# Two sets of retention tiles, and the gated merges as a phase of their own, in an eight-core retention and Hyena layer

## The chip, the cores and the metric

The kernel runs on the eight NeuronCores of one Trainium2 chip, the same program on each, with no communication between cores. Time is device time of the slowest core, in microseconds (us). Two states occur, in the kernels before and after and in 12 of the 14 experiments: in some executions the cores of one die (cores 0 to 3 or 4 to 7) get a lower clock and take some per cent longer.

Engines: PE is TensorE's matmul, PEld its weight load, DVE is VectorE, ACT is ScalarE, POOL is GpSimd, SP is the SyncE queue (it only issues DMAs here). In the traces of before and after, DVE's, ACT's and POOL's instructions run in the order in which the program issues them: on all eight cores the sequences agree by operation and size (1331, 872 and 227 instructions after the change, DMA issues included). PE's matmuls do so too (5770 after the change) on the six cores of which no records are missing. All windows below are of core 0.

## The reference, cut to what matters

One layer: normalise and modulate (`h`), one wide projection, retention (four heads), a Hyena convolution, a gated merge with output projection, then a SwiGLU FFN.

```python
h = rmsnorm(x, norm1) * (1 + scale1) + shift1
proj = h @ w_in
q, k, v, g, hu, g_ret, g_hy = jnp.split(proj, splits, axis=-1)
o, s_f, s_b = bidir_retention(qh, kh, vh, gamma_f, gamma_b, s0_fwd, s0_bwd)
y_ret = (jax.nn.silu(g) * head_groupnorm(o)) @ w_ret_o
# ... Hyena branch: z ...
y_hy = z @ w_hy_o
mix = jax.nn.sigmoid(g_ret) * y_ret + jax.nn.sigmoid(g_hy) * y_hy
x = x + gate1 * (mix @ w_out)
h2 = rmsnorm(x, norm2) * (1 + scale2) + shift2
a, bgt = jnp.split(h2 @ w_ffn_in, 2, axis=-1)
x = x + gate2 * ((jax.nn.silu(a) * bgt) @ w_ffn_out)
```

Each core has three tiles of 512 rows to bring through this: two of context (`xc`) and one of its own sample rows (`xs`). It also needs keys and values of the other half of its sample's rows, for the states. `h` is used twice: by q, k, v, g, and by the gates `g_ret`, `g_hy`.

## The kernel before

All weights of the retention phase are in SBUF together: `WR` (q, k, v, g and both gates), `WRO`, `WHO`, `WO`. There is one working set, so one `HT_R` (the transposed, modulated `h` of a tile) and one Q, K, V.

`make_hT` makes hT in 16 small stages for four blocks of 128 rows: st1 loads rows and sums squares (DVE, ACT), st2 scales (DVE), st3 transposes on PE and evicts by turns with DVE and ACT. With `defer` the stages go to a queue, and `fill(n)` puts n of them into the program wherever it is called.

```python
stages = [L(st1, 0), L(st1, 1), L(st2, 0), L(st3, 0, 0), L(st3, 0, 1), L(st1, 2), L(st2, 1), L(st3, 1, 0), L(st3, 1, 1),
          L(st1, 3), L(st2, 2), L(st3, 2, 0), L(st3, 2, 1), L(st2, 3), L(st3, 3, 0), L(st3, 3, 1)]
# st3 with hf == 1 ends with after_blk(blk): for a retention tile, K, V (and SG = silu(g)) of that block, 8 matmuls each
```

A tile then goes: Q and K by heads (`ret_rest`), retention (`ret_st`), merge (`merge_out`). Retention is a chain of eight state steps (DVE scales K, PE multiplies, DVE updates the state), then a second half of four attention items.

```python
        for k in range(max(len(ch) for ch in chains)):      # chain of ret_st
            for ch in chains:
                if k < len(ch):
                    ch[k]()
        # ... second half: s1, s23, s4 of four items ...

        def merge_out(src, g_unused, x1dst, nxt=None):
            for oc in range(8):
                # 8 + 8 matmuls for the gates from HT_R, 4 + 4 for the branches, Sigmoid, multiply, add -> MIXT
            if nxt is not None:
                nxt()
            for blk in range(4):
                # load xb
                for hf in range(2):
                    # 8 matmuls MIXT x WO
                    fill(2)
                    # gate and add; then store to x1s
```

The order of the stages, and the place where FFN weights are loaded:

```python
        merge_out(Z2T[:, :, 1024:1536], 1, ..., nxt=lambda: ret_make(xc[0:512, :], 0, True, True))
        flush()
        ret_rest(True, True)
        ret_st([([0, 1], False, False, 0, 0), ([2, 3], False, False, 1, 2)])
        merge_out(Z2T[:, :, 0:512], 0, ..., nxt=lambda: ret_make(xc[512:1024, :], 0, True, True))
        flush()
        ret_rest(True, True)
        ret_st([([0, 1], False, False, 2, 0), ([2, 3], False, False, 3, 2)])
        merge_out(Z2T[:, :, 512:1024], 0, ..., nxt=lambda: (load_wf1(), ffn_make(0, True, ...)))
```

So in the kernel before, the next tile's hT, K, V and SG are the fill of an output projection, and `load_wf1` stands ahead of the last output projection.

## Time and profile before

| | before |
|---|---|
| median of the first 6 runs | 1687.96 us |
| PE busy, share of the span | 69% |
| granted TensorE clock, mean | 0.839 on core 0 |
| changed stage, core 0 | 721 us to 1280 us |

The chain of waits of the kernel before (the work that ended last, followed back), by engine:

```profile
PE 49%; DVE 16%; issue 12%; DMA 11%; ACT 6%; POOL 3%; another core or an unknown queue 2%; SPq 1%; DVEq 1%; ACTq 0%; POOLq 0%
```

Stage windows of the kernel before. After the window come its length, then busy time and number of instructions of PE, PEld, DVE, ACT and POOL, the granted clock, the DMA share and GB/s.

```profile
721.00:766.00 45.00, 8.01 (x63) 5.75 (x64) 26.18 (x68) 7.48 (x20) 2.50 (x3) 0.55 0.85 156
766.00:804.00 38.00, 36.42 (x164) 16.47 (x165) 10.61 (x21) 10.93 (x19) 0.00 (x0) 0.95 0.03 13
804.00:828.00 24.00, 5.02 (x38) 3.32 (x38) 14.53 (x43) 3.99 (x7) 0.00 (x0) 0.57 0.00 0
828.00:855.00 27.00, 8.63 (x71) 7.09 (x73) 18.75 (x38) 6.75 (x16) 9.00 (x8) 0.56 0.00 1
855.00:900.00 45.00, 44.38 (x197) 19.75 (x198) 11.77 (x18) 11.31 (x18) 9.51 (x8) 0.96 0.00 1
900.00:948.00 48.00, 36.50 (x163) 15.45 (x167) 26.98 (x51) 18.23 (x32) 1.66 (x1) 0.93 0.30 88
948.00:968.00 20.00, 18.56 (x87) 8.23 (x86) 4.31 (x8) 6.00 (x11) 0.00 (x0) 1.00 0.40 132
968.00:1012.00 44.00, 11.46 (x92) 8.86 (x94) 26.99 (x61) 8.95 (x20) 12.07 (x12) 0.53 0.08 24
1214.00:1280.00 66.00, 27.32 (x119) 16.68 (x121) 22.75 (x42) 8.74 (x22) 9.37 (x10) 0.73 1.06 184
```

In order: the other half's state chain with the making of the sample's hT; the sample's projections; the sample's retention in two rows (chain, second half); its gate and branch matmuls; its output projection filled with the next tile's hT, K, V and SG; Q and K; a context retention; and the last tail, which is the last output projection with the FFN's hT, while FFN weights load.

In the chains and retentions PE works 5 to 12 us of 24 to 45, at a clock near 0.55: that is the idle time which the change wants. The output projection (900 to 948) holds 160 large matmuls in 48 us. (Numbers of large matmuls are those of the program: 64 of the projection and 96 of K, V and SG. The counts in the windows take in the small transposes, and some matmul records are missing from a trace.)

### The profile page before, as it was taken

Reading aid. Unit: us, or ns where it says so; the run is one execution under the profiler, and the core shown is the slowest. Engines: PE = TensorE matmul, PEld = TensorE weight load, DVE = VectorE, ACT = ScalarE, POOL = GpSimd, SP = SyncE. Lnnn points to the kernel's source line nnn. Section 1 sums busy time; section 2 is a strip of 40 time slices with the busy share of each in tenths; the row PEclk is TensorE's granted clock in tenths of the full one; section 3 lists DMA queues with packets and bytes.
Section 4 is the critical chain, followed back from the end, with each engine's and each line's share of the span. In section 5 each row is a group of like instructions: output and inputs, shape, how many; then the busy total and the mean of one; then the engine's idle time right before and its main releaser. Section 6 shows DMA issues by size and latency. Waiting matters only on the chain.

```text
span 1688.9 us, 18842 instructions; the slowest of 8 cores (1660.5 to 1688.9 us)
## 1 busy us (share of the span) xinstructions
PE 1173.3 (69%) x5677; PEld 551.9 (33%) x5776; DVE 678.5 (40%) x1303; ACT 405.3 (24%) x794; POOL 252.1 (15%) x231
## 2 busy tenths in 40 slices
PE   1613658976887963528278829764938988997996
PEld 0301113432344422214233324332423444444442
DVE  2604456534243078353634352535322134134213
ACT  1002443144023532112222322322202112111210
POOL 3100120002140054100121022002210211002002
PEclk9756679987998986658589959986969999998998
DMA  9992222332563002990002200320299912002002
GB/s 164 166 143 71 89 67 71 125 101 82 168 188 112 1 1 44 172 183 14 0 1 69 94 25 1 91 72 13 24 201 220 147 44 97 16 11 90 25 1 87
DMA packets 86346, 139.02 MB, mean 82 GB/s; under 512 B 7357, under 2 KB 57950, under 8 KB 86248
## 3 DMA queue, kind: packets, MB, share of 16 engines
q0 software_dynamic: 44976, 54.27, 20.5%
q1 hardware_dynamic: 35512, 78.30, 15.1%
q10 hardware_dynamic: 5760, 5.25, 1.0%
q8 instruction: 49, 0.80, 0.2%
q14 instruction: 49, 0.40, 0.1%
HBM read 163.73 MB, written 19.94 MB: 109 GB/s over the span
## 4 chain that ended last, share of the span: by engine, by line
PE 49%; DVE 16%; issue 12%; DMA 11%; ACT 6%; POOL 3%; another core or an unknown queue 2%; SPq 1%; DVEq 1%; ACTq 0%; POOLq 0%
PE ps L277 49%; DMA af<-x1s 3%; DVE abf L298 3%; ACT abf L295 3%; DVE af L310 3%; DVE af L298 2%; DMA af<-xc 2%; DVE abf L305 2%; ACT abf L316 1%; DMA abf<-w_in 1%; POOL af L298 1%; DVE abf L312 1%; DVE abf L303 1%; POOL abf L298 1%
## 5 line engine op out<-in xcount | busy, mean ns | idle before, releaser
L277 PE MATMUL ps<-abf 128*128 128x512 bf16 (+4 forms) x5473 | 1139.2, 365 | 404.8 <-DVE abf L298 94.4
L277 PEld LDWEIGHTS ps<-abf 128*128 128x128 bf16 (+1 forms) x5572 | 522.8, 105 | 1016.6 <-issue 584.6
L298 POOL TENSOR_TENSOR abf<-abf 128x512 bf16<-128x512 bf16 x84 | 104.5, 1259 | 527.0 <-DVE abf L298 308.9
L295 ACT ACTIVATE abf<-ps,sm 128x128 bf16<-128x128 f32 (+1 forms) x220 | 108.7, 502 | 269.3 <-DVE abf L305 201.2
L298 DVE TENSOR_TENSOR abf<-abf 128x512 bf16<-128x512 bf16 x196 | 123.7, 673 | 85.4 <-ACT abf L316 55.8
L316 ACT CAST abf<-ps 128x512 bf16<-128x512 f32 x176 | 97.7, 585 | 221.6 <-PE ps L277 151.0
L298 DVE TENSOR_TENSOR abf<-ps,af 128x512 bf16<-128x512 f32 x106 | 71.3, 689 | 192.8 <-PE ps L277 191.6
L298 DVE TENSOR_TENSOR af<-ps,af 128x512 f32<-128x512 f32 x124 | 85.0, 688 | 157.7 <-PE ps L277 138.3
L305 DVE TENSOR_SCALAR abf<-ps,sm 128x128 bf16<-128x128 f32 x176 | 70.4, 409 | 153.1 <-PE ps L277 92.5
L295 ACT ACTIVATE af<-ps 128x512 f32<-128x512 f32 x114 | 67.5, 597 | 254.9 <-PE ps L277 254.8
L298 POOL TENSOR_TENSOR af<-af 128x512 f32<-128x512 f32 x36 | 45.5, 1266 | 337.3 <-DVE af L298 194.9
L295 ACT ACT_TABLE_LOAD x34 | 43.6, 1283 | 186.8 <-DVE sm L324 112.1
L295 ACT ACTIVATE sm<-sm 128x1 f32<-128x1 f32 (+2 forms) x139 | 34.1, 248 | 211.2 <-DVE af L312 100.1
L277 PE MATMUL ps<-identf_sb,af 128*128 128x128 f32 x192 | 31.3, 319 | 53.9 <-DVE af L303 53.9
L312 DVE SCALAR_TENSOR_TENSOR af<-af 128x1024 f32<-128x1024 f32 x24 | 30.4, 1267 | 71.1 <-DMA af<-x1s 41.9
L312 DVE SCALAR_TENSOR_TENSOR abf<-af 128x1024 bf16<-128x1024 f32 x32 | 42.4, 1324 | 24.6 <-DMA af<-xc 12.6
L310 DVE SCALAR_TENSOR_TENSOR af<-af,sm,ps 128x128 f32<-128x128 f32 x96 | 33.3, 347 | 45.3 <-PE ps L277 21.7
L277 PEld LDWEIGHTS ps<-identf_sb,af 128*128 128x128 f32 x192 | 29.4, 228 | 59.8 <-issue 58.1
L298 POOL TENSOR_TENSOR abf<-af 128x512 bf16<-128x512 f32 x24 | 32.4, 1352 | 107.9 <-DVE af L298 96.2
L318 DVE CAST abf<-ps 128x512 bf16<-128x512 f32 x32 | 22.0, 691 | 57.4 <-PE ps L277 57.4
L298 DVE TENSOR_TENSOR abf<-ps,abf 128x512 bf16<-128x512 f32 (+1 forms) x52 | 27.9, 560 | 34.8 <-PE ps L277 34.7
L277 PE MATMUL ps<-af 33*64 33x512 f32 (+3 forms) x12 | 8.2, 781 | 42.2 <-DMA af<-zT_c 28.2
(54 smaller groups left out, 330.7 us busy)
## 6 DMA issues: line engine op xcount, KB each, us to landing
abf<-w_ada POOLq DMA_DIRECT2D x12, 1024.0 KB, 52.4
af<-xc SPq DMA_DIRECT2D x24, 512.0 KB, 6.1
af<-x1s SPq DMA_DIRECT2D x24, 512.0 KB, 4.1
abf<-w_in POOLq DMA_DIRECT2D x11, 1024.0 KB, 14.9
af<-xs SPq DMA_DIRECT2D x20, 512.0 KB, 3.3
abf<-w_f POOLq DMA_DIRECT2D x10, 1024.0 KB, 16.8
abf<-w_f POOLq DMA_DIRECT2D x13, 512.0 KB, 6.1
abf<-tfc_s SPq DMA_DIRECT2D x24, 256.0 KB, 3.0
```

Of the source, the lines that this page charges most:

```text
L277: P.op("pe", lambda e: e.matmul(out, lhsT=lhsT, rhs=rhs, start=start, stop=stop), reads=[lhsT, rhs], writes=[out], signal=(stop if signal ...
L295: P.op("act", lambda e: e.activation(out=out, in_=in_, func=func, **kw), reads=rd, writes=wr)
L298: P.op(eng, lambda e: e.tensor_tensor(out=out, in0=in0, in1=in1, op=op), reads=[in0, in1], writes=[out])
L303: P.op(eng, lambda e: e.tensor_scalar(out=out, in0=in0, scalar1=s1, scalar2=None, op0=op0), reads=rd, writes=[out])
L305: P.op(eng, lambda e: e.tensor_scalar(out=out, in0=in0, scalar1=s1, scalar2=s2, op0=op0, op1=op1), reads=rd, writes=[out])
L310: P.op("dve", lambda e: e.scalar_tensor_tensor(out=out, in0=in0, scalar=scalar, in1=in1, op0=op0, op1=op1), reads=rd, writes=[out])
L312: P.op("dve", lambda e: e.scalar_tensor_tensor(out=out, in0=in0, scalar=scalar, in1=in1, op0=op0, op1=op1, accum_out=accum), reads=rd, wri ...
L316: P.op("act", lambda e: e.copy(out=out, in_=in_), reads=[in_], writes=[out])
L318: P.op(eng, lambda e: e.tensor_copy(out=out, in_=in_), reads=[in_], writes=[out])
```

## The change

Its intent: give PE the next tile's projections to do while a tile's state chain waits on DVE. For that there are two working sets (`SETS`), `GOT_ALL` keeps the retention output of all three tiles, and the merges come last, in a phase of their own. The layout leaves no room for two sets and all weights together, so the gate weights (`WRG`) are loaded over the projection weights (`WRQ`) after the second retention, and hT is made a second time for each merge (`r2_make`). The diff, cut to its core:

```diff
-        WR = bfv(8704, 8, 4096)
-        HT_R = bfv(WK0, 8, 512)
+        WRQ = bfv(8704, 8, 2048)
+        def mkset(o):
+            return dict(hT=bfv(o, 8, 512), QT=bfv(o + 4096, 4, 512), KT=bfv(o + 6144, 4, 512),
+                        KTOK=bfv(o + 8192, 4, 512), VTOK=bfv(o + 10240, 4, 512), SG=bfv(o + 12288, 4, 512))
+        SETS = [mkset(25088), mkset(39424)]
+        GOT_ALL = bfv(53760, 4, 1536)
+        WRG = bfv(8704, 8, 2048)
+        WRO = bfv(71168, 4, 1024); WHO = bfv(75264, 4, 1024)
+        WO = bfv(25088, 8, 1024)
+        HT2 = [bfv(33280, 8, 512), bfv(39424, 8, 512)]
+        MIXT = bfv(43520, 8, 512)
 ...
+        # r1_make: make_hT with K, V, SG after each block, then 8 items for Q and K; all deferred
 ...
                 for ch in chains:
                     if k < len(ch):
                         ch[k]()
+                        fill(nfill)
 ...
                 s23(j)
+                fill(nfill)
 ...
-            fill(2)                       # in both state chains of the other half
+            fill(4)
 ...
+        r1_make(SA, xc[0:512, :], 0, True, True)
+        ret_st(SB_, [([0, 1, 2, 3], True, True, None, 0)], GOT_ALL[:, :, 1024:1536], 4)
+        flush()
+        r1_make(SB_, xc[512:1024, :], 0, True, True)
+        ret_st(SA, [...], GOT_ALL[:, :, 0:512], 4)
+        flush()
+        # load WRG over WRQ, and WO
+        r2_make(HT2[0], xc[0:512, :], 0, True)
+        ret_st(SB_, [...], GOT_ALL[:, :, 512:1024], 2)
+        flush()
+        merge_out(HT2[0], GOT_ALL[:, :, 0:512], ..., nxt=lambda: r2_make(HT2[1], xc[512:1024, :], 0, True))
+        flush()
+        merge_out(HT2[1], GOT_ALL[:, :, 512:1024], ..., nxt=lambda: r2_make(HT2[0], xs[0:512, :], 1, True))
+        flush()
+        merge_out(HT2[0], GOT_ALL[:, :, 1024:1536], ..., nxt=lambda: ffn_make(0, True, ...))
+        load_wf1()
```

`WF1`, the FFN's first weights, lies at 0 to 45056. In the new layout `WO` (25088 to 33280) lies inside it, and `load_wf1` comes after the last merge.

## The prediction

> **What bounds it now.** Chain of waits: PE 49%, DVE 16%, issue 12%, DMA 11%. All cores are alike (1660 to 1689 us). The changed stage runs from 663 us to 1280 us (first FFN matmul). Stage windows of core 0:
> - projections of the other half, on w_in loads: 663-721
> - state chain + hT fill: 721-766, PE busy 8 of 45, clock 0.55
> - sample projections: 766-804, PE 36 of 38
> - retentions: 804-855, 968-1012, 1125-1170; 44 to 51 us each, PE busy 11 to 14, clock about 0.55
> - merges: gate/branch matmuls about 44.5 us each, PE full; output projection + next hT/K/V/SG 48-49 us, then Q/K 19-20 us
> - last tail, 1214-1280: PE 27 of 66; it waits 14.5 and 13.5 us for x1s loads that compete with the FFN weights.
>
> So about 100 us of PE idleness in retention is the target.
>
> **What changes.** Removed from PE's serial path: 36 us of sample projections, and twice 21 us of K/V/SG (96 matmuls x 0.22 us) plus 19 us of Q/K. These become fill inside the state chains. A chain step is bound by DVE (about 3 us; eight take 20 to 24), so PE should run the fill at a warm clock: matmuls were 0.43 us apart in a cold stretch, 0.22 in the merge. [...] But fill(4) x 8 steps outnumbers the 24 items: the queue is empty after six steps, so retention's second half (about 27 us, DVE 19) stays unfilled.
> Added: hT is made three more times (each about 15 us DVE, 32 transposes, 2 MB read).
> Moved: gate weights and W_O load behind the third retention (six 1 MB loads, 6.6 us each by w_in's spacing): hidden.
> **Moved for the worse:** FFN weights. Before, they start at 1214.9, ahead of the last output projection, and end about 1354, hidden. After, W_F1 overlaps W_O, so every piece waits for the last output projection. The 12 + 11 loads took 139 us, with competition; I estimate 118 without (6.6 and 3.7 us each). FFN's first matmul waits about 13 us, its second half about 25 us for the last W_F2 piece. [...] That competition goes, worth about 25 us in the last tail.
>
> **Sum (core 0, estimates from these durations).** To 721 unchanged. Chain with sample fill 56 (before 82). Retentions with fill 86 and 80. Third with hT 67 (before 45). Merges 44.5 + 38 each (before 44.5 + 48 + 20). So the last output projection ends near 1255, give or take 25. W_F2 is there 118 later, then 62 for the rest of the first FFN tile, then 255 unchanged: about 1690. The retention side gains 50 to 70 us, mostly returned by exposed weight loads and the second hT. Chains may overlap better than I take them, so slightly lower.
>
> Predicted 1682 us, 80% range 1640 to 1718. Faster by over 2%: 0.25; within 2%: 0.58; slower by over 2%: 0.17.
>
> **What would show it.** Windows: chains 50 to 58 us with PE about 40 busy at clock 0.9; retention's second half still about 27 us; output projections about 38 us; no w_in wait at the first merge. W_F1's first issue near 1255; PE gap of 10 to 20 us before the FFN and 15 to 35 us before its second half, put down to DMA of w_f.
>
> **What would make it wrong.** In-order coupling of PE, DVE and ACT in the filled chains (70 us or more each); gate weights late because gpsimd's queue blocks retention three; or faster W_F loads and chains near 45 us (then 1640).

The sum came to 1255 (the last output projection's end) + 118 + 62 + 255 = 1690, lowered a little to 1682. The traces do show the times behind "cold" and "warm", and behind the competing loads: on core 0 before the change, the first eight matmuls of the sample's projections (from 766.6 us) start 0.43 us apart and the later ones 0.22. The two x1s loads for which PE waits in the last tail take 12.4 and 11.0 us in the chain of waits; after the change, with no weights loading at that time, they take 6.9 and 6.2.

## The result, and the profile after

| | before | after |
|---|---|---|
| median of all runs, slow ones too | 1685.55 us (20 runs) | 1790.2 us (10 runs) |
| ratio of fast runs | | 1.0637, 95% interval 1.0599 to 1.0674 |
| span of core 0 | 1688.9 us | 1779.1 us |
| PE busy, slowest core | 1173.3 us | 1205.7 us |

A ratio is the mean time of one kernel's fast runs over the mean of the other's fast runs of the same rounds, so it is not quite the ratio of the medians. Executions in which one die ran at a lower clock are left out of the means. Below, a gain between two experiments is the difference of their ratios to the kernel before; 0.01 is about 16.9 us. The intervals of both ratios go into such a difference: combined as if independent, they make it uncertain by 9 to 13 us for the experiments compared with after (an estimate).

The kernel got 6.4% slower, about 107 us. 1790 us lies far outside 1640 to 1718.

The chain of waits after, core 0:

```profile
PE 44%; DMA 16%; DVE 14%; issue 12%; ACT 7%; POOL 2%; another core or an unknown queue 2%; SPq 1%; DVEq 1%; ACTq 0%; POOLq 0%
PE ps L277 44%; DMA abf<-w_f 7%; ACT abf L295 3%; DMA af<-x1s 3%; DVE abf L298 3%; DMA af<-xc 2%; DVE af L298 2%; DVE af L310 2%; DVE abf L305 2%; DVE abf L312 1%; DMA abf<-w_in 1%; POOL af L298 1%; ACT abf L316 1%; ACT L295 1%
```

A new entry stands second: loads of `w_f`, the FFN weights, with 7% of the span.

Stage windows after, core 0, same columns as before:

```profile
709.00:783.00 74.00, 48.46 (x220) 20.86 (x224) 34.02 (x84) 22.37 (x41) 0.00 (x0) 0.80 0.09 29
783.00:864.00 81.00, 51.13 (x230) 22.48 (x234) 36.83 (x88) 27.74 (x50) 0.00 (x0) 0.75 0.08 27
864.00:892.00 28.00, 9.03 (x75) 7.33 (x74) 19.03 (x39) 7.30 (x17) 9.01 (x8) 0.50 0.00 0
893.00:965.00 72.00, 49.58 (x224) 22.87 (x228) 29.34 (x66) 24.43 (x45) 2.32 (x3) 0.78 0.13 41
965.00:993.00 28.00, 7.30 (x60) 5.99 (x60) 18.48 (x40) 7.38 (x17) 11.53 (x11) 0.50 0.04 10
994.00:1036.00 42.00, 8.83 (x68) 6.46 (x68) 21.39 (x51) 9.58 (x25) 5.77 (x7) 0.50 1.13 195
1064.00:1110.00 46.00, 44.59 (x195) 19.74 (x197) 12.50 (x21) 11.66 (x19) 10.39 (x8) 0.96 0.00 1
1110.00:1153.00 43.00, 19.96 (x88) 8.71 (x90) 21.23 (x39) 8.99 (x22) 0.80 (x1) 0.76 0.29 98
1342.00:1460.00 118.00, 94.11 (x387) 39.94 (x396) 19.05 (x30) 16.59 (x28) 18.07 (x22) 0.86 1.02 168
```

In order: the other half's chain filled with the sample tile; the sample's chain filled with the first context tile, and its second half; the first context tile's chain filled with the second context tile, and its second half; the second context tile's chain, filled with the second making of an hT; the first merge's gates and branches; the first output projection with the next second hT; and the first FFN tile's first half.

The sample's chain is more than three times as long as it was (81 us against 24), and the first context tile's retention takes 72 + 28 us against 44. The other half's chain, which held the making of an hT before too, goes from 45 to 74 us. The second halves stay at 27 to 28 us, with PE busy 7 to 9. The output projection now has 64 large matmuls instead of 160, and still takes 43 us instead of 48.

How core 0's 90 us come about, from these windows and from the PE timeline (the second row of the table takes in all filled chains, projections and second halves):

| core 0, us | before | after | difference |
|---|---|---|---|
| start of the changed stage | 721 | 709 | -12 |
| chains, projections, retentions (Q and K too) | 262 | 355 | +93 |
| gate and branch matmuls, three merges | 134 | 137 | +3 |
| three output projections | 154 | 132 | -22 |
| last output projection's end to second half of the first FFN tile | 97 | 127 | +30 |
| from there to the end | 321 | 319 | -2 |

The rows add to 1689 and 1779. The stage starts earlier after the change mostly because the stages ahead of it, which are the same, ended 8 us earlier on core 0 in that execution.

The start of the FFN after, PE alone (start, duration, engine, line, operation, tiles, count, and in brackets the idle time before it and what ended it):

```profile
1342.00 3.57 PE L277 MATMUL ps<-abf 128*128 128x512 bf16 x8 [6.17 <-DMA abf<-w_f]
1354.09 1.86 PE L277 MATMUL ps<-abf 128*128 128x512 bf16 x4 [8.52 <-DMA abf<-w_f]
1356.18 13.81 PE L277 MATMUL ps<-abf 128*128 128x512 bf16 x58 [0.22 <-issue]
1374.03 1.29 PE L277 MATMUL ps<-abf 128*128 128x512 bf16 x5 [4.04 <-DMA abf<-w_f]
```

Before, the FFN began without waits for weights: their first loads had been issued at 1214.9, 65 us ahead:

```profile
1280.07 5.31 PE L277 MATMUL ps<-abf 128*128 128x512 bf16 x12 [6.21 <-DVE abf L305]
```

But the gap ahead of the first matmul was 6.2 us before the change too, then put down to DVE. So the first of the waits above (6.17 us) costs nothing by itself on core 0; the later ones do.

### The profile page after: what moved, and what is told of

It reads as the page before. It is cut to its first block, busy times and chain, and to the rows that moved or that the text cites. A ratio compares the mean times of both kernels' runs of the same rounds, so it can differ in the third digit from the quotient of the medians.

```text
span 1784.2 us, 19444 instructions; the slowest of 8 cores (1755.5 to 1784.2 us)
## 1 busy us (share of the span) xinstructions
PE 1205.7 (68%) x5772; PEld 563.7 (32%) x5872; DVE 720.3 (40%) x1399; ACT 436.1 (24%) x870; POOL 251.5 (14%) x231
## 4 chain that ended last, share of the span: by engine, by line
PE 43%; DMA 16%; DVE 15%; issue 12%; ACT 7%; another core or an unknown queue 2%; POOL 2%; SPq 1%; DVEq 1%; ACTq 0%; POOLq 0%
PE ps L277 43%; DMA abf<-w_f 7%; ACT abf L295 3%; DMA af<-x1s 3%; DVE abf L298 3%; DVE af L298 2%; DVE abf L305 2%; DVE af L310 2%; DMA af<-xc 2%; DMA abf<-w_in 1%; POOL af L298 1%; ACT L295 1%; ACT abf L316 1%; DVE abf L312 1%
## 5 line engine op out<-in xcount | busy, mean ns | idle before, releaser
L277 PE MATMUL ps<-abf 128*128 128x512 bf16 (+5 forms) x5568 | 1171.0, 368 | 482.6 <-DVE abf L303 107.4
L277 PEld LDWEIGHTS ps<-abf 128*128 128x128 bf16 (+1 forms) x5668 | 534.1, 106 | 1115.1 <-issue 693.9
L295 ACT ACTIVATE abf<-ps,sm 128x128 bf16<-128x128 f32 (+1 forms) x268 | 130.2, 494 | 329.1 <-DVE abf L305 259.1
L305 DVE TENSOR_SCALAR abf<-ps,sm 128x128 bf16<-128x128 f32 x224 | 89.8, 409 | 191.9 <-PE ps L277 103.0
L295 ACT ACTIVATE sm<-sm 128x1 f32<-128x1 f32 (+2 forms) x163 | 40.0, 248 | 228.7 <-DVE af L312 88.0
L312 DVE SCALAR_TENSOR_TENSOR abf<-af 128x1024 bf16<-128x1024 f32 x44 | 57.1, 1297 | 40.1 <-DMA af<-xs 18.6
L318 DVE CAST abf<-ps 128x512 bf16<-128x512 f32 x32 | 22.1, 692 | 57.5 <-PE ps L277 57.5
L178 POOL DMA_DIRECT2D abf<-w_f x23 | 18.3, 797 | 142.1 <-DMA abf<-w_f 98.8
```

The source lines that it names most:

```text
L178: engine.dma_start(out=out, in_=in_, **kw).then_inc(sems[semkey], 16)
L277: P.op("pe", lambda e: e.matmul(out, lhsT=lhsT, rhs=rhs, start=start, stop=stop), reads=[lhsT, rhs], writes=[out], signal=(stop if signal ...
L295: P.op("act", lambda e: e.activation(out=out, in_=in_, func=func, **kw), reads=rd, writes=wr)
L305: P.op(eng, lambda e: e.tensor_scalar(out=out, in0=in0, scalar1=s1, scalar2=s2, op0=op0, op1=op1), reads=rd, writes=[out])
L312: P.op("dve", lambda e: e.scalar_tensor_tensor(out=out, in0=in0, scalar=scalar, in1=in1, op0=op0, op1=op1, accum_out=accum), reads=rd, wri ...
L318: P.op(eng, lambda e: e.tensor_copy(out=out, in_=in_), reads=[in_], writes=[out])
```

## The experiments

Fourteen kernels ran, each timed against the kernel before on the same chip. The theory at the start: (a) the second hT lies on the critical path, because the output projections have lost the K, V and SG matmuls under which hT was hidden; (b) FFN weights come late; (c) filling the chains gains far less than their idle time. The main rival to (a) and (b) was that the filled chains alone cost the 107 us. (The experiments ran on three chips, and the ratios are each to the kernel before on the same one.)

### FFN weights early again

```diff
-        WO = bfv(25088, 8, 1024)
+        WO = bfv(59904, 8, 1024)       # loaded after the third retention
-        MIXT = bfv(43520, 8, 512)
+        MIXT = bfv(47616, 8, 512)
-                  nxt=lambda: ffn_make(0, True, ...))
-        load_wf1()
+                  nxt=lambda: (load_wf1(), ffn_make(0, True, ...)))
```

(HT_F and UT are moved by 896 elements.)

> The kernel after, with W_O, MIXT, HT_F and UT laid elsewhere so that W_F1 no longer overlaps W_O; W_F1 is loaded ahead of the last output projection, as in the kernel before. Theory (late weights cost something, but the earlier loads compete with the x1s loads of the last tail): the w_f waits of PE before and inside the first FFN tile (about 40 us in the trace of after) go, the last output projection grows from 45 to about 65 us, and the net gain is 17 us (10 to 25), that is 1773 us. Rival (the whole wait is lost time): 35 us or more faster, 1755. Rival (weights don't matter, the FFN is bound elsewhere): within 5 us.

Measured: correct, ratio 1.0491 (1.0421 to 1.0561), so 25 us faster than after; fast runs 1769 to 1777 us. The last tail and the first FFN half, as windows of this kernel:

```profile
1289.00:1351.00 62.00, 24.30 (x119) 15.26 (x120) 21.43 (x42) 8.76 (x21) 7.64 (x9) 0.74 1.10 198
1351.00:1440.00 89.00, 88.42 (x393) 39.86 (x402) 21.48 (x35) 18.30 (x32) 11.94 (x15) 0.97 0.87 146
```

The first FFN half falls from 118 to 89 us. The tail, 55 us after the change (from 1287 to 1342), takes 62 here, with the weights loading beside its x1s loads: PE's two longest gaps in it are 13.6 and 14.8 us, against 9.0 and 8.4. (In the kernel before, which loads the weights there too, two x1s loads of the tail took 12.4 and 11.0 us in the chain of waits; after the change, with W_F1 first issued at 1330.7, they took 6.9 and 6.2.) So late weights cost 25 us net, at the upper end of what the theory gave (10 to 25). With an uncertainty of 13 us the rival's 35 is not excluded by the times alone; what speaks against it is the longer tail.

### Second hT left out (wrong on purpose)

```diff
-        r2_make(HT2[0], xc[0:512, :], 0, True)
-                  nxt=lambda: r2_make(HT2[1], xc[512:1024, :], 0, True))
-                  nxt=lambda: r2_make(HT2[0], xs[0:512, :], 1, True))
```

> Wrong result on purpose: the kernel after without the three re-makings of hT (the merges read stale tiles). Theory (the second hT is on the critical path, because the output projections have nothing left on PE to hide its latency): each of the first two output projections falls from 43 to about 20 us, the third retention's chain from 42 to about 24; 65 us faster in all, 1725. Rival (output projections are bound by their own x loads and stores on the SP queue): under 25 us faster.

Measured: wrong result; ratio 1.0167 (1.0118 to 1.0215), 79 us faster than after. The third retention's chain and the first output projection of this kernel:

```profile
989.00:1010.00 21.00, 6.81 (x52) 4.98 (x52) 11.91 (x30) 2.44 (x4) 2.63 (x3) 0.50 1.20 187
1084.00:1107.00 23.00, 21.85 (x99) 9.80 (x101) 9.93 (x15) 1.72 (x3) 0.10 (x1) 1.00 0.39 137
```

The chain falls from 42 to 21 us. The output projection falls further than the expected 20 us: the window of 23 us, with PE busy throughout, holds its 64 large matmuls (about 14 us at 0.22) and already the first 35 of the next merge's gates. So the price is better read from the start of one output projection to the start of the next. The first matmuls of the first two, after the change (two lines) and in this kernel (two lines):

```profile
1110.95 0.38 PE L277 MATMUL ps<-abf 128*128 128x512 bf16 x1 [2.04 <-POOL abf L298]
1199.88 2.93 PE L277 MATMUL ps<-abf 128*128 128x512 bf16 x9 [2.04 <-POOL abf L298]
1084.25 21.98 PE L277 MATMUL ps<-abf 128*128 128x512 bf16 x99 [0.98 <-POOL abf L298]
1141.78 21.96 PE L277 MATMUL ps<-abf 128*128 128x512 bf16 x99 [1.04 <-POOL abf L298]
```

That is 88.9 us after the change and 57.5 here; to the third output projection it is 87.3 and 58.1. So a second hT costs 21 us in the chain and 31 and 29 us in the output projections, 81 us together on core 0. Loads and stores of x do not bound the output projection.

### Fill spread over both halves

```diff
-        ret_st(SB_, [...], GOT_ALL[:, :, 1024:1536], 4)
+        ret_st(SB_, [...], GOT_ALL[:, :, 1024:1536], 2)
-        ret_st(SA, [...], GOT_ALL[:, :, 0:512], 4)
+        ret_st(SA, [...], GOT_ALL[:, :, 0:512], 2)
```

> The kernel after with 2 instead of 4 fill items per step in the first two retentions, so that the eight Q/K projections fall into the second half, which now has nothing to fill. Theory (the second half is idle time of PE that can take 14 us of matmuls): chains fall from 77 and 69 to about 62 and 55, second halves stay at 33, 28 us faster, 1762. Rival (PE takes its instructions in order, so what is put there lengthens it): second halves grow to about 45, net within 6 us.

Measured: correct, ratio 1.0516 (1.0457 to 1.0575), 20 us faster than after. Windows of the two retentions of this kernel, chain and second half:

```profile
778.00:851.00 73.00, 38.33 (x177) 16.57 (x181) 35.06 (x85) 22.71 (x41) 0.00 (x0) 0.70 0.08 29
851.00:878.00 27.00, 18.75 (x130) 10.14 (x129) 18.59 (x38) 11.23 (x25) 8.98 (x8) 0.91 0.00 1
881.00:944.00 63.00, 38.24 (x178) 17.00 (x183) 29.73 (x67) 20.11 (x36) 4.11 (x5) 0.77 0.15 51
944.00:968.00 24.00, 15.97 (x107) 8.33 (x105) 15.82 (x34) 10.65 (x24) 9.76 (x10) 0.94 0.02 3
```

By the program the second halves take in 64 large matmuls each, and they don't grow; the clock there is 0.91 and 0.94, with PE busy 18.8 of 27 and 16.0 of 24 us; after the change it was 0.50 in both, with PE busy 9.0 and 7.3 of 28. The chains lose only 8 and 9 us, not the 15 expected. This filling cost no time here; that it is because the matmuls depend on nothing that is being made at that moment is argued, not tested.

### No fill at all

```diff
-            fill(4)
-        ret_st(..., 4)
+        ret_st(..., 0)                 # the queue is flushed after each chain or retention
```

> The kernel after with no filling of the chains at all: the hT, K/V/SG and Q/K of the next tile run after the chain, alone. Theory of the prediction (the fill hides nearly the whole chain): about 20 to 24 us slower for each of three chains, +65, 1855. Rival (in-order coupling: each lump of fill and each chain step mostly wait for each other): fill saves under 8 us per chain, +0 to +25. It also measures the length of the fill alone: 73 us if the chain is fully hidden, about 50 if it isn't.

Measured: correct, ratio 1.0786 (1.0724 to 1.0849), 25 us slower than after. Windows of this kernel: the other half's chain alone, the sample tile's hT and projections alone, the sample's chain alone, the first context tile alone:

```profile
697.00:718.00 21.00, 4.28 (x32) 2.56 (x32) 12.58 (x37) 0.00 (x0) 0.00 (x0) 0.58 0.00 0
718.00:782.00 64.00, 45.72 (x192) 19.08 (x196) 24.89 (x54) 23.09 (x44) 0.00 (x0) 0.82 0.09 34
782.00:804.00 22.00, 4.95 (x36) 3.29 (x36) 12.57 (x37) 3.68 (x6) 0.00 (x0) 0.51 0.00 0
832.00:893.00 61.00, 47.24 (x196) 19.74 (x200) 19.47 (x39) 22.84 (x43) 0.06 (x1) 0.82 0.10 35
```

This is the run that shows the mis-sized term. Alone, a chain takes 21 to 22 us and a tile's fill 61 to 64. Filled, the first chain took 74 (against 85 one after the other), the second 81 (against 83) and the third 72 (against 19 + 60). So the fill is the long part: filling saved 2 to 11 us of a chain of 21, some 20 in all. The 25 us are rather more than that, probably because three of this kernel's four fast runs have a pair of cores at a clock of 0.80 to 0.81; the fourth took 1806 us, 18 above the typical fast run of after (1788). The result lies at or inside the border of the rival's range, far from the +65 which the prediction's view implies. It also rules out that the filling itself made the kernel slower: without it, it is slower still.

### Is it ScalarE's Silu?

In a filled block PE idles 3.6 us, at 728.7 to 732.3 in the trace of after. All engines of that stretch of the kernel after, weight loads left out:

```profile
727.18 1.28 ACT L295 ACT_TABLE_LOAD   x1 [4.17 <-PE ps L277]
...
728.31 0.38 PE L277 MATMUL ps<-abf 128*128 128x128 bf16 x4 [1.32 <-DVE abf L303]
728.48 0.60 ACT L295 ACTIVATE abf<-ps 128x512 bf16<-128x512 f32 x1
728.81 0.41 DVE L305 TENSOR_SCALAR abf<-ps,sm 128x128 bf16<-128x128 f32 x1 [0.64 <-PE ps L277]
729.09 1.28 ACT L295 ACT_TABLE_LOAD   x1
730.38 0.59 ACT L295 ACTIVATE sm<-sm 128x1 f32<-128x1 f32 x2
730.88 0.44 ACT L295 ACTIVATE abf<-ps,sm 128x128 bf16<-128x128 f32 x1
731.43 0.41 DVE L305 TENSOR_SCALAR abf<-ps,sm 128x128 bf16<-128x128 f32 x1 [2.21 <-ACT abf L295]
731.75 0.41 DVE L298 TENSOR_TENSOR abf<-abf 128x512 bf16<-128x512 bf16 x1
...
732.32 0.91 PE L277 MATMUL ps<-abf 128*128 128x128 bf16 x7 [3.62 <-DVE abf L298]
```

PE has done a block's first transposes (728.31). DVE evicts one quarter; the next is ACT's, but ACT first does the Silu of the block before, loads a table, and does the logarithm and exponential of st1. DVE's next eviction waits for ACT, the chain's scaling of K stands behind that eviction in DVE's order, and PE waits for the scaled K. The switch of tables takes 1.3 us here: Silu ends at 729.08, the load runs from 729.09, and the next activation starts at 730.38. Two kernels tested whether this sets the pace. The first puts Identity in place of Silu (wrong):

```diff
-                    proj_tm_blk(S, blk, 1536, S["SG"], AF.Silu)
+                    proj_tm_blk(S, blk, 1536, S["SG"], AF.Identity)
```

> Wrong result on purpose: the kernel after with Identity in place of Silu in the evictions of the gate projection. In the run without fill a chain took 21 us and the fill 62 to 64 us; filled they took 73 to 81, so little is gained by filling. Theory (ScalarE's strict order: the Silu eviction and two activation table loads of 1.28 us stand ahead of the hT evictions, and PE idles 3.6 us in each block): the gaps of 3.6 us fall to about 1.5 for each of 12 blocks, 20 to 25 us faster, 1767. Rival (the chain's own round trips between PE and DVE make the gap): under 8 us faster.

Measured: ratio 1.0524 (1.0484 to 1.0565), 19 us faster than after, just under what the theory gave; table loads fall from 38 to 20, and the gaps of 3.6 us to 2.1.

The second takes the Silu evictions of a tile together, after its hT:

```diff
                 proj_tm_blk(S, blk, 1024, S["VTOK"])
-                if full:
-                    proj_tm_blk(S, blk, 1536, S["SG"], AF.Silu)
...
-                th = [... Q ...] + [... K ...]
+                th = [... SG of four blocks, Silu ...] + [... Q ...] + [... K ...]
```

> The same theory in a correct kernel: the four Silu evictions of a tile come together after its hT instead of one in each block; table loads fall by 6 a tile. Theory: 15 to 20 us faster than after, 1772. Rival: within 6 us.

Measured: correct, ratio 1.0612 (1.0574 to 1.065), 4 us faster than after, which is inside the noise and the rival's range. The corresponding stretch of this kernel:

```profile
731.29 0.38 PE L277 MATMUL ps<-abf 128*128 128x128 bf16 x4 [3.05 <-DVE abf L303]
...
733.74 1.01 PE L277 MATMUL ps<-abf 128*128 128x128 bf16 x8 [2.07 <-DVE abf L298]
```

The gap of 3.6 us became 2.1, as with Identity, but the gap before it, 1.3 us after the change, became 3.05. The SG matmuls had kept PE busy while DVE did sums and scaling of the next rows. Table loads fell to 26, and no gain is shown: the wait moved from ACT to DVE.

### hT kept instead of made again

```diff
+        SC = dict(SB_, hT=bfv(79360, 8, 512))      # the third tile's hT in free space
-        WO = bfv(25088, 8, 1024)
+        WO = bfv(29184, 8, 1024)
-        r2_make(...)                               # all three
-        merge_out(HT2[0], ...); merge_out(HT2[1], ...); merge_out(HT2[0], ...)
+        merge_out(SA["hT"], ...); merge_out(SC["hT"], ...); merge_out(SB_["hT"], ...)
```

> A correct kernel without the second making of hT: all three tiles keep their hT (the third tile's goes to free space above W_HO), W_O moves to a place that is free by then; the FFN weights stay late. Theory (the second hT costs about 79 us, as the run that left it out on purpose showed): 79 us faster than after, 1711, output projections of 22 us. Rival (part of that gain came from wrong data or fewer loads): 1735 or more.

Measured: correct, ratio 1.0196 (1.0163 to 1.023), 75 us faster than after, close to the run that left the second hT out. So the 79 us were no effect of wrong data. One of the prediction's worries shows up here, now that nothing covers it: in the third retention PE waits 11.1 us for POOL.

```profile
1019.60 1.86 PE L277 MATMUL ps<-abf 128*128 128x128 bf16 x16 [11.09 <-POOL abf L298]
```

The same wait was 5.2 us after the change and 12.4 in the run that left the second hT out. In the program the second piece of `WO` stands ahead of the retention's work in POOL's order and waits for a gate weight to land; in the trace of after POOL waits 11.2 us for that and issues it at 1028.9. In the last kernel below (all repairs and the new order), which loads `WO` after the third retention, the wait is 5.7 us.

### All three repairs

Kept hT, early FFN weights, spread fill; the edits are those shown above.

> Kept hT, early FFN weights and the fill spread over both halves of the retentions. If the three effects (79, 24 and 20 us) add: 1667, one per cent faster than the kernel before. If the early weights are no longer worth anything because the last tail is bound by the x1s loads, or the spread fill loses to PE's order: 1685 to 1700, no faster than before.

Measured: correct, ratio 0.9882 (0.9853 to 0.9911), 1.2% faster than the kernel before, with fast runs near 1670 us. The effects add within the noise: 1.0637 less 0.0441, 0.0146 and 0.0121 is 0.9929.

### What double-buffering alone is worth

Kept hT and early weights, with the change's own fill of 4 per step:

> The kernel after with kept hT and early FFN weights, but with the fill as the change has it (4 items per step). If the costs add (ratio 1.0637 less 0.044 less 0.015): 1.005 of before, that is 1698; then double-buffering with this fill is worth nothing against the kernel before, and the whole slowdown is the second hT and the late weights. If it is 0.99 or less, the double-buffering itself gains; if 1.02 or more, it loses.

Measured: correct, ratio 0.9965 (0.9878 to 1.0053). No difference from the kernel before is shown: anything from 1.2% faster to 0.5% slower is possible.

The same without any fill:

> Kept hT and early FFN weights with no filling of the chains: all that is left of the change is the order of phases. Theory (each tile's fill takes 62 us alone, in which the kernel before hides it partly under an output projection, and a filled chain saves 0 to 11 us): about 25 us over the run before it, ratio 1.02. Rival (fill matters more once the rest is repaired): 1.04.

Measured: correct, ratio 1.0121 (1.0042 to 1.02), 26 us over the run above it. The two intervals overlap a little, and the difference is uncertain by about 20 us. As far as that goes, filling is worth about as much here as in the change as it stands (20 to 25 us).

### Is it the order of DVE's work?

The next block's sums and scaling (st1, st2) go ahead of this block's last transposes and projections:

```diff
-            stages = [L(st1, 0), L(st1, 1), L(st2, 0), L(st3, 0, 0), L(st3, 0, 1), L(st1, 2), L(st2, 1), L(st3, 1, 0), ...
+            stages = [L(st1, 0), L(st1, 1), L(st2, 0), L(st2, 1), L(st3, 0, 0), L(st1, 2), L(st3, 0, 1), L(st2, 2), L(st3, 1, 0), ...
```

> The kernel after with one change: in the making of hT, the statistics and the scaling of the next block of rows are put into the program ahead of this block's last transposes and projections, so that VectorE, which takes its instructions in order, does them while PE runs the projections. Theory (PE's gaps in each filled block are program order, not work): the gaps of 1.25 us before the transposes go in 12 blocks and the waits for x in the output projections shrink by some us each, 20 to 40 us faster than after, ratio 1.045. Rival (ScalarE's evictions or the loads set the pace): within 8 us.

> Kept hT, early weights and spread fill (0.9882 of before) with the new order of making hT. Theory: 15 to 30 us faster still, ratio 0.975. Rival: 0.985 to 0.99.

Both gave wrong results: st1 writes its scratch into the buffer of the scaled rows that the delayed transposes still had to read, and the f32 variant for the FFN reuses its row buffer in the same way. The ratios were 1.0406 (1.0296 to 1.0516) and 0.974 (0.9692 to 0.9788). The first filled chain was no shorter than after, and PE now waited there for st1 itself (4.4 us, put down to DVE at that line): the edit had brought in a wait of its own. No conclusion is drawn from the two.

Done right, with a scratch of its own and only for the bf16 hT of the retention and merge phases:

> The kernel after with the order change done right: the scratch of the squared sums has its own place, and only the bf16 hT of the retention and merge phases is reordered. Theory (program order makes VectorE late for PE): in the filled tiles the gaps before the transposes go, a filled tile falls from 73 to 77 us to about 65, and the output projections with hT from 43 to about 36; 35 us faster than after, ratio 1.043. Rival (ScalarE's Silu and table loads, the chain's round trips and the loads of x set the pace, so the wait only moves): within 10 us of after, 1.058 or more.

Measured: correct, ratio 1.051 (1.0465 to 1.0555), 21 us faster than after, between the two theories. The filled first chain, and the first output projection, of this kernel:

```profile
709.00:783.00 74.00, 48.98 (x220) 20.67 (x224) 35.08 (x84) 20.45 (x40) 0.00 (x0) 0.80 0.08 29
1098.00:1136.00 38.00, 18.63 (x88) 8.71 (x90) 20.14 (x39) 8.14 (x22) 0.07 (x1) 0.74 0.33 111
```

Most of the gain is where the second hT is made (output projections 38 instead of 43 us, the chain of the third retention 38 instead of 42). The first filled chain is as long as ever, 74 us, and so is the second with its second half (within 1 us); only the third is some 6 us shorter. So the theory mostly fails where it was meant to hold.

With all repairs:

> Kept hT, early weights, spread fill, and the order change done right. It has only three hT left to gain from. Theory: 10 to 20 us faster than the run without the order change (0.9882), ratio 0.978. Rival: 0.986 to 0.990.

Measured: correct, ratio 0.9849 (0.9795 to 0.9904), fast runs near 1664 us. It beats the kernel before by 1.5% (the interval reaches 2%, so it counts as unclear by the rule of 2%). Against 0.9882 no difference is shown, since the intervals overlap.

## Why the prediction was wrong

**What bounds it: right.** The idle time of PE in chains and retentions was there, the second halves stayed at 28 us as predicted, and putting work there gained 20 us at once (the spread fill).

**The step that failed is the sum: "Chain with sample fill 56 (before 82). Retentions with fill 86 and 80."** Measured: 74, then 81 + 28 = 109, then 72 + 28 = 100. These three terms are 61 us of the 78 us by which the last output projection ended later than predicted (1333 against 1255). The mistake in them is that the fill was counted as about 40 us of PE work which would run in the waits of the chain's steps. The fill alone takes 61 to 64 us, with PE busy only 46 to 47 of them at a clock of 0.82: it contains the making of hT, with its own round trips between PE, DVE and ACT. The 56 was below even the fill alone. The risk that the prediction named, in-order coupling with "70 us or more each", has the right number (74, 81 and 72), but most of it is the length of the fill; waiting of the two parts for each other can be at most the 10 to 20 us above that.

**"Output projections about 38 us": too small.** They took about 43, 43 and 46. With 48 before, this is the clue that was in the profile of before: taking 96 matmuls (21 us at 0.22 us) from a stage with PE busy 36.5 of 48 us brings it to 43, not to 27. The K, V and SG matmuls were almost free where they stood; what was long there was hT. The change moved them away to a place where they are paid in full, and left a second hT in their place. The run without it and the run with kept hT put the price at 79 and 75 us. The prediction's sum did charge most of this: 67 instead of 45 us for the third retention, and 38 us for each of two output projections whose 64 large matmuls alone are 14 (at 0.22 us), some 70 us together. What it had wrong is that the filled chains would earn this back.

**FFN weights: mechanism right, sizes in part.** W_F1's first piece was issued near the end of the last output projection (1330.7). The loads took from there to about 1453, 123 us with the last landing, against the estimate of 118. Waits were 6.2 us before the FFN (predicted 10 to 20; a gap of this size was there before the change too), 8.5 and 4.0 us soon after, and 11 us in sum before the second half (predicted 15 to 35). The end of the competition with the x1s loads (12.4 and 11.0 us before, 6.9 and 6.2 after) was worth 11 us in the last tail (66 to 55), not about 25. Loading early again gained 25 us, so this explains about a quarter of the slowdown.

**Gate weights hidden: right.** The first merge started without waiting for w_in. The POOL queue's blocking came to light only in the two runs without a second hT.

**The whole.** Second hT 75 to 79 us and late weights 25 us make 100 to 104 of 107. With both repaired no difference between the double-buffered kernel and the one before is shown (0.9878 to 1.0053); with fill in the second halves as well it is 1.2% faster. So the two costs are what made the kernel slower, and both were in the prediction's sum; the missing gain of the filled chains is why the sum came out too low.

**What stays open.** Why a filled chain isn't shorter than 72 to 81 us with PE busy 48 to 51 is only partly settled. Two single causes were removed, ScalarE's Silu in between and DVE's order. A correct kernel that moved the one moved the wait, and one that changed the other left the first chain at 74 us. About 12 of the 26 idle us of PE in the first filled chain lie at its two ends, where the fill has nothing for PE yet (709 to 718) or has run out (778 to 783); this is read from the trace and was not tested.

## What to carry to other kernels

Before moving work out of a stage, ask what it was hiding there: a stage that takes 48 us with 160 matmuls may take 43 with 64, and then the moved matmuls are a cost at their new place and no saving at the old. Size a fill by running it alone, not by its share of the busiest engine; here work that was itself a chain across PE, DVE and ACT saved only 2 to 11 us when it was folded into another such chain, while plain matmuls on finished data cost no time in the second halves (27 and 24 us with them, 28 and 28 without). And when a new layout puts a late weight over a buffer that is in use to the end, its load starts at the end.
